# Starting addresses of on-chip tiles: multiples of 32 bytes or multiples of 64

## The chip, the core and the metric

The kernel runs on one core of a Trainium2 chip. The metric is the device time of one execution in microseconds, a median over runs. In the profile PE is TensorE's matmul stream, PEld its weight load, DVE is VectorE, ACT ScalarE, POOL GpSimd, and SP the engine that issues most DMAs. SBUF is the on-chip memory of 128 partitions; an address here is an offset within a partition.

## The reference

One step of a two-layer backbone over 128 context tokens and 256 latent tokens of width 2048, in float32. For each layer:

```
mod = silu(c) @ w_ada + b_ada                 # shift, scale, gate
h = rmsnorm(x, norm_g) * (1 + scale) + shift
q, k, v, g_att, hy_in, g_hy = split(h @ w_in)  # 2048 -> 7168
att = attend(rope(norm(q)), rope(norm(k)) + cached k, v + cached v) * silu(g_att)
hy  = hyena(hy_in) * silu(g_hy)               # gated long convolution
x = x + gate * (concat(att, hy) @ w_out)
```

Context tokens see context only and have a modulation vector of their own. A final rmsnorm follows; the outputs are both token streams and the context's keys and values of each layer.

## The kernel before

All activations lie in SBUF as XM (128 partitions x 16 x 384 tokens). Float32 products are formed from split operands in the type fp32r: every operand is a high part (rounded by a copy to fp32r) plus a low part (the rest), and a product is three matmuls: high by high, high by low, low by high. For the normalised input the parts are hh and hl. For the weights they are hi and lo: a unit of weights is 128 x 2048 and comes in two halves of 128 x 1024, each loaded by one DMA of 512 KB into one of seven buffers raw (line 143); ScalarE copies it to hi (line 191), and VectorE subtracts to lo (line 197). The pool of hi has four buffers, that of lo three.

There are two ways in which a unit is multiplied.

- b_mm (lines 754 to 773, for k, q in two halves, and v): tokens are stationary and weights are streamed. Each matmul has a 128 x 128 piece of hh or hl as its weights and 512 columns of hi or lo as its stream. A unit has 36 of them, a group 4 units; there are 4 groups in each layer, 1152 matmuls in all.
- a_mm (lines 787 to 797, for the gates, the convolution's inputs and the output projection): weights are stationary and tokens are streamed. Each matmul has a 128 x 128 piece of hi or lo as its weights and the 384 columns of hh or hl of one row block as its stream. A unit has 48, a layer 56 units; 5376 matmuls in all.

```
767: mm(accs[g][m], hh[:, kt, ms], wh[:, k, :], start=first, stop=False)
768: mm(accs[g][m], hh[:, kt, ms], wl[:, k, :], start=False, stop=False)
769: mm(accs[g][m], hl[:, kt, ms], wh[:, k, :], start=False, stop=last)
...
795: mm(b[:, :T], wh, hh[:, kt, :], start=(kt == 0), stop=False)
796: mm(b[:, :T], wh, hl[:, kt, :], start=False, stop=False)
797: mm(b[:, :T], wl, hh[:, kt, :], start=False, stop=(kt == 15))
```

The second operand in a call is the stationary one, the third the stream. T is 384.

The rest of TensorE's work is in plain float32: the modulation (line 249, weights w_ada streamed from raw buffers, four column groups side by side), attention (lines 612 to 657), transposes (lines 262, 530, 622, 692), the convolution as products with transform matrices that lie in C (lines 501, 513, 712, 720, 742 to 745). Part of the modulation is summed on VectorE instead (lines 322 and 324, raw buffers into the accumulators pa). Other tiles: V holds vectors (conditioning, biases, gains, filter constants); P1 to P4 are large buffers that each stage uses in another way; tt, x1c, z, zz and xo are scratch from small pools; mod and asc are modulation vectors, read as scalars; eps is one word, the bias of a square root (line 388).

The order of the work is set by the program's own recording (a list of units in a fixed order, with background pieces between them by due step and cost); its tables are untouched here. In time: 0 to about 160 us, modulation of layer 0, filters, x, and the first units of k and q between them; to about 270 us the rest of q and v; then a_mm of layer 0 to about 808 us; k, q and v of layer 1 from about 816 to 950 us; a_mm of layer 1 to 1482 us; the final norm.

Tiles are placed one after another in the order in which they are made, each beginning at a multiple of 32 bytes. The single-buffer tiles come in the order XM, hh, hl, C, V, P1, P2, P3, P4, acc2, scT, ones, eps, mod, asc, raw; then follow the pools of hi, lo, tt, x1c/z/zz/xo, small vectors, and pa.

Of the kernel before, what the change touches and what calls it, by code (L numbers as in the profile page):

```python
# [10 lines left out]
F32 = mybir.dt.float32  # L11
# [40 lines left out]


V_C, V_BADA, V_NG, V_FG, V_CONV, V_QK, V_F = 0, 32, 128, 160, 176, 368, 624
V_W = 627

C_FL, C_IL, C_FC, C_IC, C_RC, C_RS, C_ID, C_TN = 0, 512, 768, 1024, 1280, 1408, 1664, 1792
C_W = 1795

INV2PI = 1.0 / (2.0 * math.pi)  # L60
MAGIC = 12582912.0
# [8 lines left out]
def step_kernel(ctx, tc, xT, vec, cst, delta, zfeat, fw, ada, wb, wc, wo, ck, cv, qk1, yT, nk, nv):  # L70
    nc = tc.nc
    pool = lambda name, bufs, **k: ctx.enter_context(tc.tile_pool(name=name, bufs=bufs, **k))
    one = pool("one", 1)
# [13 lines left out]
    hl = one.tile([128, KT, T], F32R, name="hl")  # L87
    C = one.tile([128, C_W], F32, name="C")
    V = one.tile([128, V_W], F32, name="V")
    P1 = one.tile([128, 3072], F32, name="P1")  # L90
# [4 lines left out]
    rs = acc2  # L95
    scT = one.tile([128, KT, 32], F32, name="scT")
    ones = one.tile([128, 128], F32, name="ones")
    eps = one.tile([128, 1], F32, name="eps")
    mod = [one.tile([128, 48, 2], F32, name=f"mod{l}") for l in range(NL)]
    asc = [one.tile([128, KT, 2], F32, name=f"asc{l}") for l in range(NL)]  # L100
    Hd = [[dram.tile([128, 6, 512], F32, name=f"Hd{l}{h}") for h in range(2)] for l in range(NL)]
# [946 lines left out]
def shape_constants():  # L1048
    c = np.zeros((128, C_W), np.float32)

# [85 lines left out]
```

## Time and profile before

| what | value |
|---|---|
| median of 3 runs | 1500.04 us (1499.9 to 1501.58) |
| profiled execution, its own time | 1501.41 us |
| its span, first to last instruction | 1499.6 us |
| mean granted TensorE clock | 0.989 |
| PE busy | 1467.3 us, 98% |
| DVE, ACT busy | 980.0 us, 577.3 us |
| HBM traffic | 271.49 MB read, 13.63 MB written |

A row of a group of instructions reads: line, engine, operation, target and sources by name, shapes, count, total busy time in us, mean duration of one in ns, idle time just before them with its causes. A timeline row reads: start and duration in us, engine, line, operation. A row of windows reads: stretch, length, busy time with count for each engine asked for, granted clock, DMA share, GB/s. Matmuls are pipelined: a record lasts longer than the distance to the next start, so the pace of a stream is read from starts, not from durations.

### The profile page before, as it was taken

The numbers are of one execution on the slowest core, as the hardware profiler recorded it, in microseconds if no ns is written. First come the engines' busy times: TensorE is split into PE (matmuls) and PEld (weight loads), VectorE is DVE, ScalarE is ACT, GpSimd is POOL, SyncE is SP. The second block draws the span as 40 slices with busy tenths as digits, with TensorE's granted clock in tenths as the row PEclk, the third lists the DMA queues.
The fourth block names the chain that finished last, engine by engine and source line by source line (L and its number), as shares of the span: only waits on it lengthen the run. The fifth ranks groups of instructions, "written<-read, shape, count | busy, mean of one in ns | idle before, by whom it ended". The sixth has DMA issues, their size and how long they took to land.

```text
span 1499.6 us, 20692 instructions
## 1 busy us (share of the span) xinstructions
PE 1467.3 (98%) x8020; PEld 1292.0 (86%) x8020; DVE 980.0 (65%) x1618; ACT 577.3 (38%) x959; POOL 46.3 (3%) x89
## 2 busy tenths in 40 slices
PE   9889999999999999999998999999999999999995
PEld 5345777999998988999997888899999999999995
DVE  6743566777777555687877755776777756755444
ACT  2433554555432222244233545455433232234230
POOL 1010000000000000001110000000000000000000
PEclk9999999999999999999998999999999999999998
DMA  9998556444566566556775344543455343544422
GB/s 352 356 370 303 209 200 230 162 151 159 174 219 207 200 250 218 179 205 208 249 243 179 113 136 138 176 155 129 145 175 184 137 174 126 182 170 139 156 97 85
DMA packets 78443, 286.48 MB, mean 191 GB/s; under 512 B 9638, under 2 KB 9960, under 8 KB 77832
## 3 DMA queue, kind: packets, MB, share of 16 engines
q1 hardware_dynamic: 72536, 267.19, 50.8%
q0 software_dynamic: 5808, 17.97, 3.3%
q8 instruction: 63, 1.03, 0.3%
q14 instruction: 36, 0.29, 0.1%
HBM read 271.49 MB, written 13.63 MB: 190 GB/s over the span
## 4 chain that ended last, share of the span: by engine, by line
PE 94%; DMA 4%; DVE 1%; ACT 1%; issue 0%; SPq 0%; DVEq 0%; ACTq 0%
PE acc L795 21%; PE acc L797 21%; PE acc L796 21%; PE acc L767 6%; PE acc L768 6%; PE acc L769 6%; PE adab L249 3%; DMA raw<-in_ada 2%; PE bgb L629 1%; PE bgb L612 1%; PE bgb L720 1%; PE bgb L622 1%; DMA XM<-in_xT 1%; DMA raw<-in_wb 1%; PE bgb L530 1%; DVE XM L854 1%
## 5 line engine op out<-in xcount | busy, mean ns | idle before, releaser
L795 PE MATMUL acc<-hh,hi 128*128 128x384 f32 x1792 | 613.1, 342 | 0.0
L797 PE MATMUL acc<-hh,lo 128*128 128x384 f32 x1792 | 602.4, 336 | 0.0
L796 PE MATMUL acc<-hl,hi 128*128 128x384 f32 x1792 | 602.3, 336 | 0.0
L197 DVE TENSOR_TENSOR lo<-raw,hi 128x1024 fp32r<-128x1024 f32 x288 | 350.5, 1220 | 145.1 <-issue 57.6
L191 ACT CAST hi<-raw 128x1024 fp32r<-128x1024 f32 x288 | 300.9, 1046 | 337.6 <-issue 191.8
L795 PEld LDWEIGHTS acc<-hh,hi 128*128 128x128 f32 x1792 | 336.9, 188 | 17.1 <-issue 11.2
L796 PEld LDWEIGHTS acc<-hl,hi 128*128 128x128 f32 x1792 | 337.0, 188 | 3.2 <-issue 1.0
L797 PEld LDWEIGHTS acc<-hh,lo 128*128 128x128 f32 x1792 | 336.9, 188 | 0.0
L324 DVE SCALAR_TENSOR_TENSOR pa<-raw,scT,pa 128x512 f32<-128x512 f32 x330 | 225.9, 744 | 0.0
L767 PE MATMUL acc<-hi,hh 128*128 128x512 f32 x384 | 157.0, 409 | 3.0 <-ACT hh L414 2.6
L768 PE MATMUL acc<-lo,hh 128*128 128x512 f32 x384 | 153.1, 399 | 1.5 <-DVE lo L197 1.5
L769 PE MATMUL acc<-hi,hl 128*128 128x512 f32 x384 | 152.8, 398 | 0.0
L767 PEld LDWEIGHTS acc<-hi,hh 128*128 128x128 f32 x384 | 72.9, 190 | 37.8 <-issue 14.2
L768 PEld LDWEIGHTS acc<-lo,hh 128*128 128x128 f32 x384 | 73.0, 190 | 18.1 <-DVE lo L197 2.1
L769 PEld LDWEIGHTS acc<-hi,hl 128*128 128x128 f32 x384 | 72.8, 190 | 18.3 <-DVE hl L417 0.5
L371 ACT ACTIVATE tt<-XM 128x384 f32<-128x384 f32 x48 | 24.4, 523 | 138.0 <-DVE XM L843 132.1
L249 PE MATMUL adab<-raw,scT 128*32 128x512 f32 x416 | 65.4, 617 | 8.1 <-DMA raw<-in_ada 8.1
L843 DVE SCALAR_TENSOR_TENSOR XM<-acc,mod,xo 128x256 f32<-128x256 f32 x64 | 23.8, 412 | 64.5 <-PE acc L797 64.5
L686 DVE SCALAR_TENSOR_TENSOR z<-acc,V,z 128x255 f32<-128x255 f32 (+1 forms) x64 | 25.2, 414 | 36.9 <-ACT z L682 35.7
L686 DVE SCALAR_TENSOR_TENSOR XM<-acc,V,XM 128x255 f32<-128x255 f32 (+1 forms) x64 | 25.1, 414 | 30.3 <-ACT XM L682 29.1
L249 PEld LDWEIGHTS adab<-raw,scT 128*32 128x32 f32 x416 | 9.8, 108 | 38.0 <-issue 18.4
L686 DVE SCALAR_TENSOR_TENSOR x1c<-acc,V,x1c 128x255 f32<-128x255 f32 (+1 forms) x64 | 25.2, 414 | 26.2 <-ACT x1c L682 25.1
(160 smaller groups left out, 1061.0 us busy)
## 6 DMA issues: line engine op xcount, KB each, us to landing
raw<-in_ada SPq DMA_DIRECT2D x192, 512.0 KB, 5.0
raw<-in_wc SPq DMA_DIRECT2D x160, 512.0 KB, 3.9
raw<-in_wb SPq DMA_DIRECT2D x64, 512.0 KB, 4.8
raw<-in_wo SPq DMA_DIRECT2D x64, 512.0 KB, 4.1
Hd<-P POOLq DMA_DIRECT2D x24, 256.0 KB, 8.6
P<-Hd SPq DMA_DIRECT2D x4, 1536.0 KB, 8.7
XM<-in_xT SPq DMA_DIRECT2D x4, 768.0 KB, 9.9
xo<-in_xT POOLq DMA_DIRECT2D x16, 192.0 KB, 3.8
```

The lines of the kernel that those rows point to most:

```text
L191: nc.scalar.copy(u.hi[h], u.raw[h])
L197: nc.vector.tensor_tensor(u.lo[h], u.raw[h], u.hi[h].bitcast(F32), ALU.subtract)
L249: mm(part[32 * t:32 * t + 32, :], scT[:, kc * 4 + t, :], u.raw[t // 2][:, (t % 2) * 512:(t % 2 + 1) * 512], start=(kc == 0), stop=(kc == 3))
L324: nc.vector.scalar_tensor_tensor(out=acc, in0=w, scalar=sc, in1=acc, op0=ALU.mult, op1=ALU.add)
L371: nc.scalar.activation(sq[:, :T], XM[:, kt, :], AF.Square)
L686: nc.vector.scalar_tensor_tensor(out=out[:, o:o + n], in0=bank[:, i:i + n], scalar=w(k), in1=out[:, o:o + n], op0=ALU.mult, op1=ALU.add)
L767: mm(accs[g][m], hh[:, kt, ms], wh[:, k, :], start=first, stop=False)
L768: mm(accs[g][m], hh[:, kt, ms], wl[:, k, :], start=False, stop=False)
L769: mm(accs[g][m], hl[:, kt, ms], wh[:, k, :], start=False, stop=last)
L795: mm(b[:, :T], wh, hh[:, kt, :], start=(kt == 0), stop=False)
L796: mm(b[:, :T], wh, hl[:, kt, :], start=False, stop=False)
L797: mm(b[:, :T], wl, hh[:, kt, :], start=False, stop=(kt == 15))
```

## The change

Three numbers differ. V gets 640 words in place of 627, C 1808 in place of 1795, and eps is a tile of 16 words of which the first is used. The arrays that are loaded into V and C are wider by the same 13 words of zeros. No instruction is added, removed or moved on any engine; the two loads of V and C are 128 x 640 and 128 x 1808 instead of 128 x 627 and 128 x 1795.

```
-V_W = 627
+V_W = 640
...
-C_W = 1795
+C_W = 1808
...
-    eps = one.tile([128, 1], F32, name="eps")
+    eps = one.tile([128, 16], F32, name="eps")[:, 0:1]
```

What it does to the starting addresses, as the remainder by 64 in the program as built:

| tile | before | after |
|---|---|---|
| XM, hh, hl, C | 0 | 0 |
| V | 32 | 0 |
| P1, P2, P3, P4, acc2, scT, ones, eps | 0 | 0 |
| mod, asc (both layers) | 32 | 0 |
| raw (7 buffers) | 32 | 0 |
| hi (4 buffers), lo (3 buffers) | 32 | 0 |
| tt, x1c, z, zz, xo | 32 | 0 |
| small vectors (red, r, ss, mx, z of the softmax) | 32 and 0 by turns | 0 and 32 by turns |
| pa (2 accumulators) | 32 | 0 |

C's 7180 bytes took 7200 (a multiple of 32), V's 2508 took 2528, and eps took 32; now they take 7232, 2560 and 64, all multiples of 64. Everything behind eps moves up by 96 bytes, P1 to ones by 64. Every buffer of hi, lo and raw has 4096 bytes, so all buffers of a pool have the same remainder.

## The prediction

> **What bounds the kernel now.** I read the page first: busy times, slices, chain.
>
> ```profile
> span 1499.6 us, 20692 instructions
> ...
> PE 1467.3 (98%) x8020; PEld 1292.0 (86%) x8020; DVE 980.0 (65%) x1618; ACT 577.3 (38%) x959; POOL 46.3 (3%) x89
> ...
> PE 94%; DMA 4%; DVE 1%; ACT 1%; issue 0%; SPq 0%; DVEq 0%; ACTq 0%
> ```
>
> TensorE is the chain for 94% of the span. DMA owns 4%, in the first 150 us. VectorE and ScalarE follow. So a change of layout counts if it changes how fast matmuls stream, or how fast the first loads land; anything on the other engines is covered by TensorE.
>
> The change moves no instruction; it moves addresses. By the list of tiles in the section on the change, the split weights (hi, lo), the raw loads, tt, x1c, z, zz, pa, mod and asc start 32 bytes past a multiple of 64 now; XM, hh, hl, C, P1 to P4, scT and ones start at one already. Both kinds stand side by side in one trace, so I looked for pairs: the same operation on a half-line tile and on an aligned one. These are groups of instructions by line and shape.
>
> ```profile
> L197 DVE TENSOR_TENSOR lo<-raw,hi 128x1024 fp32r<-128x1024 f32 x288 | 350.5, 1220 | 145.1 <-issue 57.6 <-ACT hi L191 46.4 <-PE acc L768 29.4
> ...
> L795 PEld LDWEIGHTS acc<-hh,hi 128*128 128x128 f32 x1792 | 336.9, 188 | 17.1 <-issue 11.2 <-ACT tt L805 2.5 <-ACT z L682 0.8
> ...
> L767 PEld LDWEIGHTS acc<-hi,hh 128*128 128x128 f32 x384 | 72.9, 190 | 37.8 <-issue 14.2 <-ACT hh L414 4.5 <-ACT hi L191 1.4
> ...
> L703 DVE TENSOR_TENSOR P<-P,P 128x1024 f32<-128x1024 f32 x8 | 9.7, 1218 | 0.0
> ...
> L503 ACT ACTIVATE tt<-bgb 128x512 f32<-128x512 f32 x8 | 4.7, 591 | 7.1 <-PE bgb L501 7.0
> ...
> L514 ACT ACTIVATE P<-bgb 128x512 f32<-128x512 f32 x8 | 4.7, 584 | 3.9 <-PE bgb L513 3.9
> ```
>
> VectorE: 1220 ns with all three operands on a half line (lo, raw, hi), 1218 ns with all aligned (P). ScalarE: 591 against 584 ns for a half-line and an aligned target. Weight loads: 188 ns from hi (half line), 190 ns from hh (aligned). So three kinds of access show at most 7 ns. For the loads I take the mean over windows in the start phase, the last two columns being DMA share and GB/s.
>
> ```profile
> 25.00:33.00 8.00, 8.00 (x44) 2.61 (x42) 7.86 (x13) 1.78 (x3) 0.49 (x1) 1.00 1.03 415
> 35.00:49.00 14.00, 11.14 (x37) 2.98 (x35) 8.04 (x14) 6.24 (x14) 3.99 (x9) 1.00 1.03 416
> ```
>
> In the first window transfers into XM (aligned) share the engines with raw loads, in the second almost all are into raw (half line): 415 and 416 GB/s, both with the engines full.
>
> What is left is the moving operand, the one streamed through the array. Three kinds of rows tell its pace. The first block is the timeline of TensorE in the projections a_mm (aligned stream hh/hl of 384 columns, half-line weights), the second of b_mm (half-line stream hi/lo of 512 columns, aligned weights); the start in its second row is the 52nd after that in its first.
>
> ```profile
> 1348.77 0.34 PE L795 MATMUL acc<-hh,hi 128*128 128x384 f32 x1
> ...
> 1349.81 0.34 PE L795 MATMUL acc<-hh,hi 128*128 128x384 f32 x1
> ```
>
> ```profile
> 827.66 0.39 PE L769 MATMUL acc<-hi,hl 128*128 128x512 f32 x1
> ...
> 839.79 0.39 PE L767 MATMUL acc<-hi,hh 128*128 128x512 f32 x1
> ```
>
> The third is the chain of waits, where plain fp32 matmuls (two passes over their columns, everything aligned) stand in groups.
>
> ```profile
> 289.79 1.29 PE bgb L629 x6
> ...
> 1219.88 3.43 PE bgb L720 x8
> ```
>
> a_mm: six starts in 1.04 us, 173.3 ns each. b_mm: 52 in 12.13 us, 233.3 ns each. Plain fp32: L629 has 256 columns and takes 1.29/6 = 215 ns, L720 has 512 and takes 3.43/8 = 429 ns. The difference is 214 ns for 256 columns in two passes, 0.418 ns for a column in one pass, and 1 ns stays over as a fixed part. At that pace a single pass over 384 columns would take 161.5 ns and over 512 columns 215.0 ns. So a_mm's matmuls have a surplus of 11.8 ns and b_mm's one of 18.3 ns. The difference is 6.5 ns, and 64 bytes (16 columns) of a one-pass stream are 16 x 0.418 = 6.7 ns. A stream of 2048 bytes that starts on a half line touches 33 stretches of 64 bytes, not 32. The surplus that b_mm has beyond a_mm is the price of that one stretch, to two tenths of a nanosecond.
>
> **The change part by part.** *Stream of b_mm (hi, lo).* Estimate from the rows above: the matmul falls from 233.3 to 226.8 ns, 6.5 ns less. How many of them lie on the path comes from windows of line 767 alone (its two partners 768 and 769 have as many).
>
> ```profile
> 80.00:120.00 40.00, 11.35 (x25) 0.91 1.00 385
> 120.00:160.00 40.00, 17.93 (x44) 1.00 0.82 287
> 160.00:200.00 40.00, 20.31 (x51) 1.00 0.50 174
> 200.00:280.00 80.00, 29.43 (x73) 1.00 0.61 209
> 800.00:960.00 160.00, 77.97 (x192) 0.97 0.41 140
> ```
>
> Before 160 us the DMA share is 1.00 and 0.82: the units arrive late, and a matmul saved there only waits longer. I count (25 + 44) x 3 = 207 matmuls there at nothing; were that cover gone they would bring 1.3 us more. After it stand (51 + 73 + 192) x 3 = 948 on the path: 948 x 6.5 = 6.2 us. Next in line there is the split of weights on VectorE, 2 x 1.22 us (the row of line 197) for a unit of 36 matmuls (36 x 233.3 ns = 8.4 us), so nothing takes the saving back. The lower bound of this price is nothing, the upper all 18.3 ns (17.3 us, in a rival below). Between them: if a_mm's surplus of 11.8 ns grows with the length of the stream, 512 columns have 15.7 of their own, 2.6 ns is left to the half line, and 948 x 2.6 = 2.5 us. I take 6.5 because that difference is, within the reading of the rows, one stretch.
>
> *Weights of a_mm (hi, lo).* Nothing: the load takes 188 against 190 ns, and it lies beside the stream of the matmul ahead. The timeline where a unit of a_mm gives way to attention says the same.
>
> ```profile
> 289.28 0.34 PE L796 MATMUL acc<-hl,hi 128*128 128x384 f32 x1
> 289.45 0.34 PE L797 MATMUL acc<-hh,lo 128*128 128x384 f32 x1
> 289.63 1.46 PE L629 MATMUL bgb<-P,P 128*128 128x256 f32 x6
> ```
>
> The last a_mm matmul streams while weights from P (aligned) are loaded, and still holds the array 0.18 us, as the others do. So its surplus doesn't come from half-line weights. If it did, up to 5376 x 11.8 = 63.4 us would be there (1792 on each of three lines): a rival below.
>
> *Loads.* C and V grow by 13 words in each of 128 partitions, 6.7 KB each, 13.3 KB together: at 416 GB/s 0.03 us, in the start phase. The raw loads land at the same rate on either alignment: nothing. If they were a tenth slower than aligned ones, the 4% of the chain that DMA has would give 6 us; the rows exclude that.
>
> *Scratch, mod, asc, eps.* VectorE and ScalarE pairs differ by 2 and 7 ns; ScalarE is busy 38% of the span, and both run under TensorE. Nothing, in either direction.
>
> The sum is -6.2 us. The profiled execution took 1501.41 us, 1.8 more than its span; against it that is 1495.2. The median of the runs is 1500.04, 1493.8 after it: I predict 1494. About 0.2% (3 us) is what a measurement of this kernel can tell from no change.
>
> **The rivals.** *No effect (1500).* The surplus of fp32r streams could belong to the stream alone, for example 9/8 of 0.418 ns a column less one constant, which fits 173.3 and 233.3 as well as my reading does. For it: all other pairs are equal. Against: nothing but the coincidence of 6.5 with 6.7. The time is 1500, give or take the spread of the three runs (1499.9 to 1501.6). The Trainium skill speaks for this one: the page "SBUF — State Buffer", section "Specifications (TRN2)", gives lines of 16 bytes, of which an address at 32 past a multiple of 64 is as much a start as the multiple itself. By that rule the gain is nothing and the time stays 1500. The trace does show that reads care for such lines, in the one tile read with a step of two words (L692).
>
> ```profile
> L622 PEld LDWEIGHTS bgb<-C,P 128*128 128x128 f32 x96 | 11.5, 141 | 1.5
> ...
> L692 PEld LDWEIGHTS bgb<-C,zz 128*128 128x128 f32 x48 | 7.0, 182 | 0.0
> ```
>
> 182 ns against 141 for contiguous words: touching twice the bytes costs, so my stretch is possible; which size it has, no row shows. (zz is a half-line tile too, but so is hi, whose contiguous loads take no longer than aligned ones.) The case between, 2.5 us off (1497.5), counts as no change.
>
> *All surplus goes (1419).* If half-line weights slow a_mm and half-line streams slow b_mm, both fall to 0.418 ns a column: 5376 x 11.8 + 948 x 18.3 = 63.4 + 17.3 = 80.7 us, 1419. Against it are the 0.18 us at 289.45 and the equal weight loads. The Trainium skill's page "TensorE: Matmul & The Clock Gate", section "Back-to-back issue gap", states N/2.4 + 2.5 ns, 162.5 and 215.8 here; an estimate by that page is 75 us less, 1425.
>
> *Slower (1536).* The weight load of the next matmul starts in the same instant as the stream.
>
> ```profile
> 1349.81 0.34 PE L795 MATMUL acc<-hh,hi 128*128 128x384 f32 x1
> 1349.81 0.19 PEld L796 LDWEIGHTS acc<-hl,hi 128*128 128x128 f32 x1
> ```
>
> Now one begins on a whole line and the other on a half; afterwards both begin on whole lines. If the two reads are kept apart by that and collide once per matmul afterwards, a_mm pays one stretch, 5376 x 6.7 = 36 us: 1536. It outweighs the gain from 6.2 / 5376 = 1.2 ns a matmul. Against: L629 and L720 have stream and weights aligned and no surplus, though at half the pace, where there is room.
>
> **How the numbers follow.** One stretch less in b_mm: 0.40, 1494 (1492 to 1497 by itself: 8 ns and the hidden ones at one end, half of the price at the other). Length-bound part only, 1497.5: 0.06. No effect, 1500: 0.34. All surplus goes: 0.09. Collision: 0.11. Faster by over 0.2% is 0.40 + 0.09 = 0.49, within it 0.34 + 0.06 = 0.40, slower 0.11. The range holds the first three cases, 0.80: from 1490 (the first case's end and some spread) to 1502 (the slowest run shown).
>
> **What would show it.** Right: starts in b_mm about 226.8 ns apart, those in a_mm still 173.3, layer 1's projections (800 to 960 us) some 3.7 us shorter (576 x 6.5) and those after 160 us in layer 0 some 2.4 us; VectorE, ScalarE and weight-load means where they were; the DMA windows still at 415 GB/s. Wrong: b_mm still at 233.3 (no effect), a_mm off 173.3 in either direction (the weights matter, for good or ill), or a difference that sits in the first 150 us (the loads matter).

## The result, and the profile after

| | before | after |
|---|---|---|
| median | 1500.01 us (4 runs, 1499.9 to 1501.58) | 1511.0 us (4 runs, 1509.95 to 1514.41) |
| profiled execution, its span | 1501.41, 1499.6 us | 1511.98, 1510.2 us |

The ratio is 1.0075, with a 95% interval from 1.0056 to 1.0093: the change makes the kernel slower by 11 us, where 6 us faster was forecast. The page of the kernel after has the same counts of instructions on each engine; the row gives busy time, share of the span and count:

```profile
PE 1478.4 (98%) x8020; PEld 1305.0 (86%) x8020; DVE 980.1 (65%) x1618; ACT 576.9 (38%) x959; POOL 46.2 (3%) x89
```

VectorE and ScalarE have the busy time that they had (980.0 and 577.3 us before); TensorE has 11.1 us more. Where these lie is read from four places that both chains of waits have: the first attention product of layer 0, the sum of squares at its end, the first attention product of layer 1, and the final norm. First the kernel before, then after.

```profile
269.88 1.29 PE bgb L612 x4
...
809.33 1.29 PE bgb L386 x10
...
966.02 1.29 PE bgb L612 x4
...
1487.46 2.73 DVE XM L854 x5
```

```profile
268.88 1.29 PE bgb L612 x4
...
813.94 1.83 PE bgb L386 x10
...
970.09 1.29 PE bgb L612 x4
...
1498.02 2.73 DVE XM L854 x5
```

At the first place the kernel after is 1.0 us ahead, at the second 4.6 us behind, at the third 4.1, at the last 10.6. So the stretches with b_mm (up to 270 us, and 809 to 966 us) got shorter, by 1.0 and 0.5 us, and those with a_mm longer, by 5.6 and 6.5 us. The two shorter ones hold other work too, so what the stream of b_mm itself gained is read from the distances of its starts below. The start phase with its loads lost nothing. The timeline of the kernel after in a_mm, and then in b_mm:

```profile
1420.03 0.34 PE L795 MATMUL acc<-hh,hi 128*128 128x384 f32 x1
...
1421.79 0.34 PE L796 MATMUL acc<-hl,hi 128*128 128x384 f32 x1
```

```profile
874.49 0.40 PE L768 MATMUL acc<-lo,hh 128*128 128x512 f32 x1
...
877.97 0.40 PE L768 MATMUL acc<-lo,hh 128*128 128x512 f32 x1
```

The a_mm rows are ten starts apart, 1.76 us, 176.0 ns each (173.3 before); the b_mm rows 15 starts, 3.48 us, about 232 ns (233.3 before). Taken over all starts of the trace that follow one of their kind without another's work between them (within 190 ns for a_mm, 5242 of them, within 250 ns for b_mm, about 1060), the means are 175.89 after 173.45 and 232.58 after 233.24 ns. That is 5242 x 2.44 - 1060 x 0.66 = 12.8 - 0.7 = 12.1 us, which is the result to about 1 us. In a_mm the single distances now repeat every five starts (176, 173, 174, 175, 182 ns), where they were 173 and 174 before.

So the loss lies in a_mm, where the moved tiles are the weights and to which the prediction had given nothing; b_mm, where they are the stream and on which it had put 6.2 us, gave 0.7.

### The profile page after: what moved, and what is told of

It is laid out like the page before. It is cut to its first block, busy times and chain, and to the rows that moved or that the text cites. A ratio compares the mean times of both kernels' runs of the same rounds, so it can differ in the third digit from the quotient of the medians.

```text
span 1510.2 us, 20692 instructions
## 1 busy us (share of the span) xinstructions
PE 1478.4 (98%) x8020; PEld 1305.0 (86%) x8020; DVE 980.1 (65%) x1618; ACT 576.9 (38%) x959; POOL 46.2 (3%) x89
## 4 chain that ended last, share of the span: by engine, by line
PE 93%; DMA 4%; DVE 1%; ACT 1%; issue 0%; SPq 0%; DVEq 0%; ACTq 0%
PE acc L795 21%; PE acc L796 21%; PE acc L797 21%; PE acc L767 6%; PE acc L769 6%; PE acc L768 6%; PE adab L249 3%; DMA raw<-in_ada 3%; PE bgb L629 1%; PE bgb L612 1%; PE bgb L720 1%; PE bgb L622 1%; DMA XM<-in_xT 1%; DMA raw<-in_wb 1%; PE bgb L530 1%; DVE XM L854 1%
```

## The experiments

Every kernel below that computes the layers has the instructions of the kernel before in the same order; only starts differ (and those built on the changed kernel keep its two wider loads). What they have in common is named here once: the **difference** is the start of hi (or lo, whose buffers are multiples of 512 bytes away) less the start of hh (hl likewise), as a remainder by 512. It was 32 bytes before and is 128 after the change. I began with two theories. One: the two reads of a matmul, weights and stream, disturb each other when they start on the same half of 64 bytes. The other: each operand's own start counts. A third was that other tiles (raw, scratch, mod) are at fault.

**Split weights alone, and all the others alone.** The first kernel moves hi and lo alone to a multiple of 64; the second is the changed kernel with hi and lo alone moved back off it.

The same two lines are added to the kernel before and to the changed kernel.

```
+    pool("gap1", 1).tile([128, 8], F32, name="gap1"); hip = pool("hip", HIB)
...
+    pool("gap2", 1).tile([128, 8], F32, name="gap2"); tp = pool("tp", 3)
```

> Only hi and lo start at a multiple of 64, all other tiles as before (raw, tt, mod and so on at 32); V, C and eps as before. If the slowdown belongs to the split weights (either theory of them), the a_mm starts are 176.0 ns apart as after the change, b_mm 232.5, and the time is 1511. If it belongs to raw, scratch or mod and asc (writes by other engines or by DMA), a_mm stays at 173.4, b_mm at 233.2, and the time at 1500.

> The changed kernel, with hi and lo alone moved back to 32 past a multiple of 64. Split weights at fault: a_mm 173.4, b_mm 233.2, 1500. Other tiles at fault: 176.0, 232.5, 1511.

The first took 1506.57 us, ratio 1.0034 (1.0021 to 1.0047); the second 1517.35, ratio 1.0108 (1.0091 to 1.0125). Neither theory had expected either number. Of the first, the timeline in a_mm; of the second, the same.

```profile
1419.67 0.34 PE L797 MATMUL acc<-hh,lo 128*128 128x384 f32 x1
...
1439.98 0.34 PE L795 MATMUL acc<-hh,hi 128*128 128x384 f32 x1
```

```profile
1419.72 0.34 PE L795 MATMUL acc<-hh,hi 128*128 128x384 f32 x1
...
1439.86 0.34 PE L795 MATMUL acc<-hh,hi 128*128 128x384 f32 x1
```

115 starts in 20.31 us are 176.6 ns, 114 in 20.14 us 176.7 ns. Over the whole trace the second has 176.66 ns as well, but the first 175.19: its stretches of a_mm don't all run at one pace, of which more below. The second kernel has hi and lo at 32 past a multiple of 64, as before, and is the slowest of all. So whether hi and lo start at a multiple of 64 is not the point. What the two kernels do differ in from the one before is the difference: 64 and 160 bytes. Whether the other tiles have a part, these two leave open, since the first is slow without them moved and the second with them; the kernel with difference 192 below settles it.

**hh and hl moved.** Two more kernels put hh and hl 32 bytes on, with hi and lo at 0 and at 32 past a multiple of 64. Both have the lines shown; the first has gap1 and gap2 as well.

```
+    one.tile([128, 8], F32, name="gap3"); hh = one.tile([128, KT, T], F32R, name="hh")
...
+    one.tile([128, 8], F32, name="gap4"); C = one.tile([128, C_W], F32, name="C")
```

> hh and hl at 32 past a multiple of 64, hi and lo at 0, so the two reads of a matmul again start on different halves, the other way round. Theory of the meeting reads (only the difference of the two starts counts): a_mm back at 173.4 and the time at 1500 or a little below, since b_mm now streams from a whole line. Theory of the weights' own start (a_mm is slow when its weights start at 0): a_mm 176.0, 1510 or more.

> hh and hl at 32 as well as hi and lo. Theory of the meeting reads: a_mm 176.0 and the time near 1511, as after the change, with every start off a multiple of 64. Theory of the weights' own start: a_mm 173.4, and the time 1500.

The first (difference 96) took 1499.82 us, ratio 0.9996 (0.9987 to 1.0005), with a_mm at 173.42 and b_mm at 233.29 ns on average: what the theory of the two reads expected, though b_mm streams from a multiple of 64 and gains nothing. Its b_mm:

```profile
880.19 0.40 PE L767 MATMUL acc<-hi,hh 128*128 128x512 f32 x1
...
889.99 0.40 PE L767 MATMUL acc<-hi,hh 128*128 128x512 f32 x1
```

42 starts in 9.80 us, 233.3 ns. The second (difference 64) took 1503.37 us, ratio 1.0019 (1.0010 to 1.0029), where one theory expected 1511 and the other 1500. Its b_mm is the telling part:

```profile
879.74 0.39 PE L767 MATMUL acc<-hi,hh 128*128 128x512 f32 x1
...
887.98 0.39 PE L767 MATMUL acc<-hi,hh 128*128 128x512 f32 x1
```

36 starts in 8.24 us, 228.9 ns. Over all starts it has 229.17, and the kernel with split weights alone at 0 had 229.19, with hi, lo, hh and hl each 32 bytes lower and the same difference of 64. In a_mm the two have 174.65 and 175.19, so there something else has a part too.

**A sweep of the difference.** The next kernel measures the disputed thing by itself: one line per group of 32 matmuls.

```
for k in range(32): mm(b[:128, :384], at(w, r, 128, k, 128), at(h, 0, 384, k, 384), ...)   # A
for k in range(32): mm(b[:128, :512], at(h, 0, 128, k, 128), at(w, r, 512, k, 512), ...)   # B
```

> The layers are left out: this kernel only runs groups of 32 fp32r matmuls from two tiles, h and w, that hold one loaded unit of weights, and writes back its inputs. Each group has a line of its own; form A streams 384 columns of h with 128 columns of w as weights (like a_mm), form B streams 512 columns of w with 128 columns of h as weights (like b_mm), and the start of w lies 0 to 496 bytes (steps of 16) past a multiple of 512 from that of h; some groups move both starts by the same amount, some take 32 columns of weights, some other lengths of the stream. Theory that the difference of the two starts decides: the sweep gives again what the full kernels had at each difference (A and B in ns: 32 bytes 173.4 and 233.2, 64 bytes 174.7 to 175.2 and 229.2, 96 bytes 173.4 and 233.3, 128 bytes 175.9 and 232.6, 160 bytes 176.7 and 234.2), both starts moved together change nothing, 512 bytes more repeat it, and with 32 columns of weights (a quarter of the reading) the pace falls toward 161.5 and 215 ns. Theory that each start counts by itself: moving both starts by 32 bytes changes the pace as moving one does. Theory that the surplus belongs to the stream: 32 columns of weights change nothing.

The timeline shows each group as one row: start, duration of the whole group, line.

```profile
24.88 5.71 PE L97 MATMUL acc<-h,w 128*128 128x384 f32 x32
...
69.48 5.79 PE L113 MATMUL acc<-h,w 128*128 128x384 f32 x32
...
203.61 7.45 PE L161 MATMUL acc<-w,h 128*128 128x512 f32 x32
...
218.30 7.63 PE L165 MATMUL acc<-w,h 128*128 128x512 f32 x32
...
233.23 7.50 PE L169 MATMUL acc<-w,h 128*128 128x512 f32 x32
...
752.97 5.73 PE L321 MATMUL acc<-h,w 128*32 128x384 f32 x32
...
812.44 5.71 PE L341 MATMUL acc<-h,w 128*32 128x384 f32 x32
```

Lines 97 and 113 are A at differences 0 and 128: 80 ns more for the same work. Lines 161, 165 and 169 are B at 0, 32 and 64: 7.45, 7.63 and 7.50. The pace of each group, from its last 24 starts, in ns:

| difference | 0 | 32 | 64 | 96 | 128 | 160 | 192 | 224 |
|---|---|---|---|---|---|---|---|---|
| A | 173.3 | 173.3 | 173.3 | 176.7 | 176.0 | 176.7 | 173.3 | 173.3 |
| B | 226.7 | 233.3 | 228.9 | 233.3 | 233.3 | 234.3 | 233.3 | 233.3 |

From 256 to 480 bytes the same 16 numbers come again, to 0.2 ns. So the period is 256 bytes, not 64. Both starts moved together by 32, 64, 128 or 256 bytes (at differences of 32, 64 and 128) give the same pace, B at 128 excepted, with 232.7 or 233.3; moved by 16 or 48 bytes they don't (A at 32: 176.7 in place of 173.3; line 257, A at 128: 176.7 in place of 176.0). The theory that each start counts by itself has fallen for starts that are multiples of 32, which is what a tile's start is here. Two expectations of the theory that won failed. A at 64 and 96 bytes is not what the full kernels had. And with 32 columns of weights the pace never falls toward 161.5: at a difference of 32 (line 321) A stays at 173.3, so the surplus of 11.8 ns over 161.5 doesn't come from how much of the weights is read. What the difference adds to it is another matter: at 128 bytes, 32 columns of weights take A from 176.0 back to 173.3 (line 341 against line 113) and B from 233.3 to 231.0. At 64 bytes they make B slower, 231.7 in place of 228.9. These are single groups: they show that the amount of weights counts there, and not how.

**The operand order of the kernel, and what stands ahead.** At 64 and 96 bytes the sweep's A and the full kernels disagree. The next kernel runs the order of a_mm at each difference, entered in five ways.

```
for k in range(2): mm(b[:, :256], raw..., XM..., ...)        # 0, 1, 2, 5 or 8 of plain fp32
for k in range(60): mm(b[:, :384], (hi, hi, lo)[k % 3]..., (hh, hl, hh)[k % 3]..., ...)
```

> The layers are left out. Groups of fp32r matmuls in the operand order of a_mm (hi, hi, lo against hh, hl, hh) and b_mm, at differences of 0 to 224 bytes in steps of 32, each entered from several numbers of plain fp32 matmuls (0, 1, 2, 5, 8) ahead; then other lengths of the stream, and plain fp32 matmuls at three differences. If the difference alone sets the pace: each difference has one pace whatever stands ahead. If the pace is a state that the first matmuls fall into: differences 64 and 96, where the first sweep and the full kernels disagree (A 173.33 against 174.7 to 175.2, 176.67 against 173.4), show 173.33 in some groups and 175 to 177 in others. Plain fp32 at half the pace shows no dependence (215.8 and 429 ns for 256 and 512 columns).

Two groups at difference 64 that differ only in what runs ahead (another group of fp32r matmuls; one plain fp32 product); shown are the starts of the 8th and of the last of 60.

```profile
67.45 0.34 PE L105 MATMUL acc<-hl,hi 128*128 128x384 f32 x1
76.64 0.33 PE L105 MATMUL acc<-hh,lo 128*128 128x384 f32 x1
...
187.43 0.34 PE L137 MATMUL acc<-hl,hi 128*128 128x384 f32 x1
196.44 0.34 PE L137 MATMUL acc<-hh,lo 128*128 128x384 f32 x1
```

52 starts: 9.19 us or 176.7 ns in one, 9.01 us or 173.3 ns in the other. So at some differences the pace is a state into which a group falls within its first matmuls. For a_mm's order that is so at 64 (two groups at 176.7, two at 173.3, one at 174.7) and at 224 (173.3 or 176.7); at 0, 32, 96 and 192 all five groups have 173.3, at 128 all have 175.9 to 176.1 and at 160 all 176.7. At 96 the expectation failed, then: no group had the 176.7 of the first sweep, and no run shows why. For b_mm's order three groups each have 226.7 to 227.0 at 0, 228.8 to 229.0 at 64, 232.4 to 233.3 at 128, 234.3 at 160, and 233.2 to 233.5 at the rest.

The full kernels show the same state. In the two with difference 64, each of the 68 stretches of a_mm that run without a break for more than 20 starts keeps one of three paces, 173.3, 174.6 or 176.7 ns, from its 9th start to its end. Of all starts, 1847, 785 and 2610 lie at these paces where the split weights alone were moved (mean 175.19), and 2584, 974 and 1684 where hh and hl were moved too (mean 174.65). All three occur after the same work (eight stretches behind 16 rows of the attention product of line 612, in the kernel with hh and hl moved), so what picks the state is not the kind of work ahead alone.

Plain fp32, at half the pace, doesn't care: 384 columns at differences 0 and 128, 8 matmuls that the profile shows as 16 rows.

```profile
964.34 5.32 PE L401 MATMUL acc<-XM,raw 128*128 128x384 f32 x16
...
995.30 5.32 PE L413 MATMUL acc<-XM,raw 128*128 128x384 f32 x16
```

**The best difference, and a difference of 192 with every start on a multiple of 64.** By the sweep, 0 is the only place where both forms are fastest. The kernel before is 32 bytes off it, the 32 bytes that eps takes. One kernel puts eps into one more word of V's tile; the other is the changed kernel with 64 more bytes ahead of hi.

```
-    V = one.tile([128, V_W], F32, name="V")
+    V = one.tile([128, V_W + 1], F32, name="V")
-    eps = one.tile([128, 1], F32, name="eps")
+    eps = V[:, V_W:V_W + 1]
-        nc.sync.dma_start(out=V, in_=vec)
+        nc.sync.dma_start(out=V[:, 0:V_W], in_=vec)
```

```
+    pool("gap1", 1).tile([128, 16], F32, name="gap1"); hip = pool("hip", HIB)
```

> The kernel before with its one word eps placed in the last column of V's tile, so that 32 bytes fall away ahead of the split weights and hi, lo start at the same remainder by 256 (and by 512) as hh, hl. Theory that the difference of the two starts by 256 decides: the sweep has 173.33 ns for A and 226.67 ns for B at difference 0, the best of both, so a_mm stays at 173.4, b_mm falls from 233.2 to 226.7, and with 948 matmuls on the path the time falls by 6.2 us, to 1494. Theory of equal halves of 64 bytes meeting (the slower rival of the prediction): difference 0 is the worst place, a_mm 176 or more, 1511 or more.

> The changed kernel with 64 more bytes ahead of hi: every start is a multiple of 64 as in the changed kernel, but the difference to hh is 192 bytes, not 128. Theory of the difference by 256: the sweep has 173.33 and 233.3 there, so 1500. Theory of the multiples of 64 (any pair of starts at whole lines meets): 176.0, 232.6 and 1511.

Difference 0 took 1495.26 us, ratio 0.9968 (0.9957 to 0.9980): faster than both kernels, by 4.9 us against the one before and 15.7 against the changed one. Difference 192 took 1499.7, ratio 0.9998 (0.9989 to 1.0007): all tiles that the change put on multiples of 64 are on them here, and nothing is lost. The timelines: b_mm and a_mm of difference 0, and a_mm of difference 192.

```profile
903.88 0.39 PE L769 MATMUL acc<-hi,hl 128*128 128x512 f32 x1
...
907.73 0.39 PE L768 MATMUL acc<-lo,hh 128*128 128x512 f32 x1
...
1419.81 0.33 PE L796 MATMUL acc<-hl,hi 128*128 128x384 f32 x1
...
1439.92 0.33 PE L795 MATMUL acc<-hh,hi 128*128 128x384 f32 x1
```

```profile
1419.82 0.34 PE L797 MATMUL acc<-hh,lo 128*128 128x384 f32 x1
...
1439.93 0.34 PE L796 MATMUL acc<-hl,hi 128*128 128x384 f32 x1
```

b_mm has 17 starts in 3.85 us, 226.5 ns. a_mm has 116 in 20.11 us in both kernels, 173.4 ns.

All full kernels together, by difference; the sum is 5242 times what a_mm's mean has over 173.45 plus 1060 times what b_mm's has over 233.24:

| kernel | difference | a_mm, ns | b_mm, ns | sum, us | time less before, us |
|---|---|---|---|---|---|
| eps in V's padding | 0 | 173.54 | 227.73 | -5.4 | -4.9 |
| before | 32 | 173.45 | 233.24 | 0 | 0 |
| split alone at 0 | 64 | 175.19 | 229.19 | +4.8 | +5.9 |
| h at 32, split at 32 | 64 | 174.65 | 229.17 | +2.0 | +2.7 |
| h at 32, split at 0 | 96 | 173.42 | 233.29 | -0.1 | -0.8 |
| after | 128 | 175.89 | 232.58 | +12.1 | +11.0 |
| all but split at 0 | 160 | 176.66 | 234.24 | +17.9 | +16.7 |
| after, 64 bytes more | 192 | 173.31 | 233.32 | -0.6 | -0.4 |

The two paces account for each time to within 1.2 us.

## Why the prediction was wrong

- *What bounds the kernel, and where to look.* Right: only the pace of fp32r matmuls changed. VectorE, ScalarE, loads and scratch came out at nothing, as costed; the kernel with difference 192, in which all these tiles stand as after the change, took 1499.7 us and settles that.
- *Stream of b_mm, -6.2 us.* Wrong, and the step that failed is the reading of 6.5 ns as the price of one half-line stretch. A stream that starts at a multiple of 64 still has 233.3 ns (differences 96 and 192), and one that doesn't has 229.2 (h and split both at 32). The difference of the two operands decides, and the change took it to 128, where b_mm has 232.6: 0.7 us gained of the 6.2 forecast. That 226.7 ns does occur, at difference 0, 6.6 less than 233.3 and with a kernel at 1495.26, is luck: its reason was another, and the change doesn't go there.
- *Weights of a_mm, nothing.* Wrong, and this is where the 11 us are. I compared weight loads by their durations (188 and 190 ns), which stay the same in the kernel after (188 in a_mm, and 189 to 190 in b_mm), and took that for proof. The duration of a load said nothing of what it does to the stream beside it. The check at 289.45 was as weak: one start-to-start distance, 0.18 us to two digits, can't tell 173.3 from 176 ns, and it asked whether the surplus over 161.5 goes, not whether it can grow. The rows of plain fp32, at half the pace, couldn't tell either: they don't depend on the difference at all (5.32 us at 0 and at 128). Measured, this term is 5242 x 2.44 ns = 12.8 us, and not nothing. The prediction's own sign for it, a_mm off 173.3, is what came.
- *The rivals.* The slower one named the kind of thing, two reads of one matmul that depend on where each starts relative to the other, and had its place (a_mm) right. Its price, a whole stretch of 6.7 ns, was too high by nearly three times: 2.4 ns. Its condition was wrong too: equal halves of 64 bytes are not it, since difference 0 is the best place and 192 costs nothing, and the period is 256 bytes. *No effect* fell with 1511.0 us. *All surplus goes* fell: no difference took a_mm below 173.3 ns. And the surplus isn't in proportion to the length of the stream, on which the case between and the nine eighths of *no effect* were built: at difference 0 the second sweep has 119.9, 146.7, 173.3 and 227.1 ns for 256, 320, 384 and 512 columns, which is 0.417 ns a column and 13 to 14 ns over at each (448 and 480 columns stand out, with 206.7 and 216.7).
- *The chances.* 0.11 was given to slower, and 1536 to its time, with a range that ended at 1502. The trace of before had only one difference in its fp32r matmuls, 32 bytes. A rival that turns on a quantity of which a trace shows one value has no bound from that trace, and deserved more than 0.11.

Not settled: why 256 bytes, and what in the array or the memory does it. That the two reads share something is argued from the dependence on their difference. It isn't shown, and the groups with 32 columns of weights don't point one way: less to read took the extra time of A away at 128 bytes, changed nothing at 32 and made B slower at 64. What picks one of the three paces of a_mm at difference 64 was not found. Steps below 16 bytes were not tried.

## What to carry to other kernels

When matmuls run in fp32r, treat the two operands' start addresses as a pair: sweep the difference over 256 bytes in a kernel of its own, in the operand order of the real one, and then set it by padding or by where a small tile is put. Rounding each tile up to a tidy boundary sets such a difference without looking at it: the rounding here did, and lost 11 us. And any change of a small tile ahead of the big ones moves everything behind it, so a time that shifts by half a per cent after an unrelated edit may be this.

## What the runs showed of the hardware that was not expected

- The pace of fp32r matmuls depends on the difference of the two operands' starts, as a remainder by 256 bytes, as long as both starts are multiples of 32: 173.3 to 176.7 ns for 384 columns, 226.7 to 234.6 for 512 (the most is at 208 bytes, in the sweep's steps of 16).
- At some differences several paces are stable for the same instructions (173.3, 174.6 and 176.7 ns at 64 bytes); an unbroken stretch keeps the one that it fell into.
- Distances repeat in short cycles: five starts at 128 bytes for 384 columns, 176, 173, 174, 175, 182 ns.
- The Trainium skill's page "TensorE: Matmul & The Clock Gate", section "Step-by-step: what each phase is for", states that the two read ports of the engine are independent, so that loading the next weights takes no read bandwidth from the running matmul. For plain fp32 the runs agree (16 rows of 384 columns in 5.32 us at differences 0 and 128). For fp32r the weights' start does count beside the stream's, 5.71 against 5.79 us for 32 matmuls of the sweep, and there the measurement decides; whether read bandwidth is what is lost, no run shows.
